# The FFN gates' shifted transfers on the loads' queue, the conv weights loaded spread, the gate products placed between weight splits

## The chip, the cores and the metric

The kernel runs on one core of a Trainium2 chip. The metric is the device time of one execution in microseconds (us); lower is better. One execution of the kernel before was also recorded by the hardware profiler, and all views of the profile below come from that one.

## What is computed

The reference is a decoder trunk of two layers on 256 tokens of width 2048, everything in float32. Layer 0 is a Conformer convolution block, layer 1 an attention block; each is followed by a feed-forward block with a short convolution in its gate. That feed-forward block, with an inner width of 5632, is what the change touches:

```python
def conv_ffn(h, w_in, w_conv, w_out):
    g, u = jnp.split(h @ w_in, 2, axis=-1)
    g = causal_dwconv(g, w_conv)
    return (jax.nn.silu(g) * u) @ w_out

# in each of the two layers, after its convolution or attention block
x = x + conv_ffn(rms_norm(x, ffn_norm_g[layer]), ffn_w_in[layer], ffn_w_conv[layer], ffn_w_out[layer])
```

The convolution is causal and three tokens wide, with one weight for each token distance and column: the gate of token t is a weighted sum of the columns at t, t-1 and t-2.

## The kernel before

**Matrix products.** `linear` (L116 to L165) multiplies the 256 tokens (two halves of 128) by 512 columns of a weight matrix. It walks over the rows of the weights in pairs of 128, a pair being called a chunk here: a 512 KB load into a tile `raw`, issued by SyncE (SP, L134); a ScalarE (ACT) copy that rounds it into the tile `wh` (L138); a VectorE (DVE) subtraction that keeps the rest in `wl` (L144); and twelve TensorE (PE) matmuls, for each of the two rows of the pair and each half of the tokens one with `wh` and the high part of the tokens (L161), one with `wl` (L162) and one with the tokens' low part (L163). `raw`, `wh` and `wl` have four buffers each, so that loads and splits run up to four chunks ahead of the matmuls: a buffer of `wh` or `wl` comes free when the matmuls of the chunk four earlier are done, and a buffer of `raw` when the split of the chunk four earlier is done. A product with 2048 rows has 8 chunks and 96 matmuls.

**The feed-forward block.** `ffn` (L475) runs twice, for l = 0 and l = 1. Its first part goes in 11 groups j of 512 gate columns; each group has two calls of `linear`, one for the gates (`mm_g`, L487) and one for the other half (`mm_u`, L499), so 192 matmuls. Between them stands the convolution along the tokens, which lie on the partitions:

- ACT evicts the gates into `g[0]` (L489, two instructions of 512 columns).
- For the distances d = 1 and 2 the gates are moved down by d partitions into `g[d]`, by three transfers each inside the core's memory (L491, L492, L493): 112 rows, the 15 or 14 that are left, and the d rows that cross from the first half of the tokens to the second. ACT issues all six, on a queue that nothing else uses at that time.
- The 3 x 512 weights of the convolution come as 6 KB into one partition of `wc` on GpSimd's (POOL's) queue (L485), and a GpSimd instruction copies them to all partitions (L486). `wc` has one buffer.
- DVE multiplies `g[1]`, `g[2]` and `g[0]` by their weights (L495) and adds them up (L497), ACT takes the silu (L498), DVE multiplies by the other half (L501), and eight transposes on PE with their splits turn the result for the second part (`turn`, L178, L193, L194).

The second part (L504, L505) multiplies the turned result with `ffn_w_out` in four calls of `linear` with 22 times 2 rows each, and runs `after_ffn0` or `after_ffn1` on each outcome; the latter lets SP issue the stores of the result (L620) between the loads.

**What sets the order.** No order is written out for the FFN. A planner plays the whole program in a model of time as it builds it and puts each instruction into its engine's queue when the model has its inputs and buffers ready; of two that are ready the one that is earlier in the program goes first. Each queue then runs strictly in that order on the chip: an instruction that waits holds up all behind it on its engine, also the transfers that SP or ACT have yet to issue. `tc.issue_after(i)` adds a constraint: what is traced under it on the engine of `i` stands behind `i` in the queue.

Of the kernel before, what the change touches and what calls it, by code (L numbers as in the profile page):

```python
# [10 lines left out]
ALU = mybir.AluOpType  # L11
AX = mybir.AxisListType

P = 128
S = 256
D = 2048
F = 5632
# [9 lines left out]
def kernel(  # L27
# [5 lines left out]
    nc = tc.nc  # L33
# [77 lines left out]
        nc.scalar.activation(warm, ones, AF.Sigmoid)  # L111


    previous = []

    def linear(w, xt, n0, name, lo_engine=None, gain=None, feed=None, nn=512, halves=1, after=None, beside=None,  # L116
               turned=None):

        lo_engine = lo_engine or (lambda c: nc.vector)
        nk = w.shape[0] // P
        acc = ps.tile([P, 2, 512], F32, tag="mm", name=f"mm_{name}", bufs=2)
        wv = w.rearrange("(c p) (h n) -> p c h n", p=P, h=halves)
        for c0 in range(0, nk, 2):
            if feed:
                feed(c0)  # L130
            raw = wp.tile([P, 2, 512], F32, tag="raw", name="raw", bufs=4)[:, :, :nn]
            for h in range(halves):
                k = nn // halves
                nc.sync.dma_start(raw[:, :, h * k:(h + 1) * k], wv[:, c0:c0 + 2, h, n0:n0 + k])  # L134
            wh = wp.tile([P, 2, 512], F32R, tag="wh", name="wh", bufs=4)[:, :, :nn]
            wl = wp.tile([P, 2, 512], F32R, tag="wl", name="wl", bufs=4)[:, :, :nn]
            if gain is None:
                i = nc.scalar.activation(wh, raw, AF.Copy)  # L138
                if beside:
                    with tc.issue_after(i.ins):  # L140
                        beside()
                e = lo_engine(c0 // 2)
                with tc.issue_after(after[e]) if after else ExitStack():
                    i = e.tensor_tensor(wl, raw, wh.bitcast(F32), op=ALU.subtract)  # L144
                if after:
                    after[e] = i.ins
            else:
                for i in range(2):
                    g = prm[:, gain, c0 + i:c0 + i + 1]
                    nc.scalar.activation(wh[:, i, :], raw[:, i, :], AF.Copy, scale=g)  # L150
                    nc.vector.scalar_tensor_tensor(wl[:, i, :], raw[:, i, :], g, wh[:, i, :].bitcast(F32),  # L151
                                                   op0=ALU.mult, op1=ALU.subtract)
            behind = turned if turned and c0 == 4 else previous[0] if turned and c0 == 0 else None
            with tc.issue_after(behind) if behind else ExitStack():
                for i in range(2):
                    c = c0 + i
                    xh, xl = xt[c // 4]
                    for b in range(2):
                        th = xh[:, c % 4, b * P:(b + 1) * P]
                        tl = xl[:, c % 4, b * P:(b + 1) * P]  # L160
                        nc.tensor.matmul(acc[:, b, :nn], th, wh[:, i, :], start=(c == 0), stop=False)  # L161
                        nc.tensor.matmul(acc[:, b, :nn], th, wl[:, i, :], start=False, stop=False)  # L162
                        mm = nc.tensor.matmul(acc[:, b, :nn], tl, wh[:, i, :], start=False, stop=(c == nk - 1))  # L163
        previous[:] = [mm.ins]
        return acc  # L165
# [68 lines left out]
    def project(g, xt, feed=None, beside=None, turned=None):  # L234

        k0, n = GROUPS[g][0] * P, len(GROUPS[g]) * P
        b1 = cp.tile([P, 512], F32, tag="b1", name="b1", bufs=1)
        with tc.high_priority(offset=URGENT):
            acc = linear(conv_w_pw1[0], xt, k0, f"pw1_{g}", lambda c: nc.vector if c in ON_DVE[g] else nc.gpsimd,
                         feed=feed, nn=2 * n, halves=2, beside=beside, turned=turned)  # L240
        for i in range(2):
            nc.sync.dma_start(b1[:, i * n:(i + 1) * n],
                              conv_b_pw1[0:1, i * D + k0:i * D + k0 + n].to_broadcast([P, n]))
        return b1, acc
# [87 lines left out]
    with tc.tile_pool(name="stage", bufs=1) as stage:  # L332
        xt = []
# [8 lines left out]
        def feed(c0):  # L342
            if c0 % 4 == 0:
                xt.append(turn(xg[c0 // 4], G_CONV, xp, "a", c0 // 4))
            elif c0 < 12:
                n = c0 // 4 + 1
                nc.sync.dma_start(xg[n], xv[:, :, n * 512:(n + 1) * 512])
            else:
                turn_taps()
            if c0 == 6:  # L350

                for i, j in ((0, 16), (16, CW)):
                    nc.sync.dma_start(taps[i:j], conv_w_dw[0, i:j])

        b1, acc = project(0, xt, feed)
# [5 lines left out]
    with tc.tile_pool(name="diag", bufs=2) as dp:  # L361
# [18 lines left out]
        def beside():  # L380
            for _ in range(3):
                next(building, None)
# [15 lines left out]
        for g in range(len(GROUPS)):  # L398
            if g:
                b1, acc = project(g, xt, beside=beside if g >= 2 else None, turned=turned)  # L400
# [31 lines left out]
    with tc.tile_pool(name="y", bufs=1) as yp:  # L432
# [25 lines left out]
        xt = []  # L458
        rms = Rms("f0")
        after = {nc.vector: last[0], nc.gpsimd: last_pool[0]}  # L460
        for n in range(NG):
            acc = linear(conv_w_pw2[0], yt, n * 512, f"pw2_{n}",
                         None if n else (lambda c: nc.vector if c < 3 else nc.gpsimd), after=None if n else after)
            b2 = yp.tile([P, 512], F32, tag="b2", name="b2", bufs=2)
            nc.sync.dma_start(b2, conv_b_pw2[0:1, n * 512:(n + 1) * 512].to_broadcast([P, 512]))
            with tc.issue_after(after[nc.gpsimd]):
                nc.gpsimd.tensor_tensor(xg[n], xg[n], b2[:, None, :].to_broadcast([P, 2, 512]), op=ALU.add)
            add_residual(acc, n)
            xt.append(turn(xg[n], G_F0, xp, "a", n))
            rms.add(n)  # L470
# [4 lines left out]
    def ffn(l, xt, r, after):  # L475
        with tc.tile_pool(name=f"h{l}", bufs=1) as hp:

            g = [hp.tile([P, 2, 512], F32, name=f"g{d}") for d in range(3)]
            wc = hp.tile([P, 3, 512], F32, name="wc")
            for d in (1, 2):  # L480
                nc.gpsimd.memset(g[d][:d, 0, :], 0.0)
            ht = []
            for j in range(NJ):
                cols = slice(j * 512, (j + 1) * 512)
                nc.gpsimd.dma_start(wc[0:1], ffn_w_conv[l:l + 1, :, cols])  # L485
                nc.gpsimd.partition_broadcast(wc, wc[0:1])  # L486
                acc = linear(ffn_w_in[l], xt, j * 512, f"g{l}_{j}")  # L487
                for b in range(2):
                    nc.scalar.activation(g[0][:, b, :], acc[:, b, :], AF.Copy, scale=r[:, b:b + 1])  # L489
                for d in (1, 2):  # L490
                    nc.scalar.dma_start(g[d][d:d + 112], g[0][:112])  # L491
                    nc.scalar.dma_start(g[d][d + 112:], g[0][112:P - d])  # L492
                    nc.scalar.dma_start(g[d][:d, 1, :], g[0][P - d:, 0, :])  # L493
                for d in (1, 2, 0):
                    nc.vector.tensor_tensor(g[d], g[d], wc[:, 2 - d:3 - d, :].to_broadcast([P, 2, 512]), op=ALU.mult)  # L495
                for d in (1, 2):
                    nc.vector.tensor_tensor(g[0], g[0], g[d], op=ALU.add)  # L497
                nc.scalar.activation(g[0], g[0], AF.Silu)  # L498
                acc = linear(ffn_w_in[l], xt, F + j * 512, f"u{l}_{j}")  # L499
                for b in range(2):  # L500
                    nc.vector.scalar_tensor_tensor(g[0][:, b, :], acc[:, b, :], r[:, b:b + 1], g[0][:, b, :],  # L501
                                                   op0=ALU.mult, op1=ALU.mult)
                ht.append(turn(g[0], None, hp, "h", j))
            for n in range(NG):  # L504
                acc = linear(ffn_w_out[l], ht, n * 512, f"out{l}_{n}")  # L505
                after(n, acc, g[1 + n % 2])
# [4 lines left out]
    def after_ffn0(n, acc, spare):  # L511
        add_residual(acc, n)
        xt_kv.append(turn(xg[n], None, xp, "a", n))
        rms.add(n)

    ffn(0, xt, r, after_ffn0)
    r = rms.done()


    with tc.tile_pool(name="attn", bufs=1) as ap:  # L520
# [62 lines left out]
        for n in range(NG):  # L583
# [3 lines left out]
            acc = linear(w_kv, xt_kv, D + n * 512, f"v_{n}", gain=G_KV)  # L587
# [6 lines left out]
            for c2 in range(2):  # L594
                po = tp("po")
                for c in range(2):
                    i = 2 * c2 + c
# [7 lines left out]
        xt = []  # L605
        rms = Rms("f1")
        for n in range(NG):
            acc = linear(w_o[0], ot, n * 512, f"o_{n}")
# [7 lines left out]
    def after_ffn1(n, acc, spare):  # L616
        for b in range(2):
            t = spare[:, b, :]
            nc.vector.tensor_tensor(t, acc[:, b, :], xg[n][:, b, :], op=ALU.add)
            nc.sync.dma_start(ov[:, b, n * 512:(n + 1) * 512], t)  # L620

    ffn(1, xt, r, after_ffn1)


# [28 lines left out]
```

## Time and profile before

| | us |
|---|---|
| median of 3 runs | 2202.88 (2202.12 to 2204.95) |
| the profiled execution, its own time | 2218.21 |
| its span, first to last instruction | 2216.4 |

The profiled execution took 15.33 us longer than the median, and 1.8 us of its time lie around the span. How to read it: rows give the time in us from the start of the span, then the duration, the engine, the line of the kernel, and what the instruction writes and reads (`g<-mm_g,r_f` writes tile `g` from `mm_g` and `r_f`); in brackets stands how long the engine was idle before it and what ended that. ACTq and SPq are the sequencers of ACT and SP that issue transfers; such an issue isn't counted as busy time, but the engine's queue goes on only behind it. PE's matmuls are pipelined: a matmul is shown with some 0.39 us, while the next starts 0.23 us after it; PE's pace is therefore read from the starts, and short waits don't show as idle time.

### The profile page before, as it was taken

To read this page: it belongs to the slowest core of one execution; us is meant where nothing else is said; L and a number is where in the kernel's file an instruction comes from. 1 tells how busy PE (TensorE), PEld (TensorE's weight loads), DVE (VectorE), ACT (ScalarE), POOL (GpSimd) and SP (SyncE) were. 2 spreads that over 40 slices of the span, in tenths; PEclk is the share of its full clock that TensorE was granted. 3 is DMA by queue.
4 is the path that set the end of the run, shared out by engine and by line. 5 is a ranking of instruction groups with operands and counts; after the bars stand their busy time and mean duration, and the time that the engine had idled before them with its cause. 6 is when DMAs were issued, how large, how long until landed. Compare 5 with 4: busy or idle time off the path is not lost.

```text
span 2216.4 us, 27040 instructions
## 1 busy us (share of the span) xinstructions
PE 2173.0 (98%) x9951; PEld 1800.9 (81%) x9951; DVE 1395.1 (63%) x1760; ACT 1058.1 (48%) x1443; POOL 303.8 (14%) x207
## 2 busy tenths in 40 slices
PE   8999799999999999999999999999999999999999
PEld 7788688888788888888888888888788888888887
DVE  6999865665666655444566666555666566654443
ACT  6775454444444444444465565544344444443342
POOL 5898501000010000000011001000100000000000
PEclk9999899999999999999999999999999999999999
DMA  7664356777667676555655555567676667766664
GB/s 224 179 205 121 103 192 188 213 215 209 201 209 218 204 211 202 190 190 190 191 182 170 171 177 166 170 187 211 200 218 209 211 198 211 216 208 203 205 201 132
DMA packets 240620, 426.80 MB, mean 193 GB/s; under 512 B 16777, under 2 KB 56091, under 8 KB 240455
## 3 DMA queue, kind: packets, MB, share of 16 engines
q1 hardware_dynamic: 231906, 401.72, 58.5%
q10 hardware_dynamic: 7876, 23.21, 3.9%
q8 instruction: 78, 1.28, 0.2%
q14 instruction: 56, 0.46, 0.1%
q0 software_dynamic: 704, 0.14, 0.0%
HBM read 399.97 MB, written 2.10 MB: 181 GB/s over the span
## 4 chain that ended last, share of the span: by engine, by line
PE 78%; DVE 10%; DMA 7%; issue 2%; ACT 1%; ACTq 1%; POOL 1%; SPq 0%; DVEq 0%; POOLq 0%
PE mm_g L163 7%; PE mm_g L161 7%; PE mm_g L162 7%; PE mm_out L161 7%; PE mm_out L163 7%; PE mm_out L162 7%; DVE acc L281 4%; PE mm_u L162 4%; PE mm_u L163 4%; DMA g<-g 3%; PE mm_u L161 3%; DMA raw<-in_ffn_w_in_dram 2%; DVE wl L144 2%; PE mm_pw L163 2%; PE mm_pw L161 2%
## 5 line engine op out<-in xcount | busy, mean ns | idle before, releaser
L144 DVE TENSOR_TENSOR wl<-raw,wh 128x1024 fp32r<-128x1024 f32 (+1 forms) x595 | 749.1, 1269 | 568.4 <-ACT wh L138 568.4
L138 ACT ACTIVATE wh<-raw 128x1024 fp32r<-128x1024 f32 (+1 forms) x664 | 689.4, 1048 | 815.1 <-PE mm_out L163 272.0
L162 PE MATMUL mm_u<-wl,ah 128*128 128x512 f32 x704 | 276.4, 393 | 11.3 <-DVE wl L144 11.1
L161 PE MATMUL mm_g<-wh,ah 128*128 128x512 f32 x704 | 276.0, 392 | 0.0
L162 PE MATMUL mm_g<-wl,ah 128*128 128x512 f32 x704 | 275.9, 392 | 0.0
L161 PE MATMUL mm_out<-wh,hh 128*128 128x512 f32 x704 | 274.4, 390 | 0.0
L163 PE MATMUL mm_g<-wh,al 128*128 128x512 f32 x704 | 274.3, 390 | 0.0
L163 PE MATMUL mm_out<-wh,hl 128*128 128x512 f32 x704 | 274.2, 389 | 0.0
L162 PE MATMUL mm_out<-wl,hh 128*128 128x512 f32 x704 | 274.1, 389 | 0.0
L163 PE MATMUL mm_u<-wh,al 128*128 128x512 f32 x704 | 274.1, 389 | 0.0
L161 PE MATMUL mm_u<-wh,ah 128*128 128x512 f32 x704 | 274.0, 389 | 0.0
L151 DVE SCALAR_TENSOR_TENSOR wl<-raw,prm,wh 128x512 fp32r<-128x512 f32 x192 | 137.6, 747 | 68.6 <-ACT wh L150 68.4
L150 ACT ACTIVATE wh<-raw,prm 128x512 fp32r<-128x512 f32 x192 | 127.9, 716 | 92.3 <-PE mm_v L163 28.7
L162 PEld LDWEIGHTS mm_u<-wl,ah 128*128 128x128 f32 x704 | 132.1, 188 | 47.1 <-DVE wl L144 20.1
L144 POOL TENSOR_TENSOR wl<-raw,wh 128x1024 fp32r<-128x1024 f32 (+1 forms) x69 | 156.8, 2290 | 36.5 <-ACT wh L138 36.3
L161 PEld LDWEIGHTS mm_u<-wh,ah 128*128 128x128 f32 x704 | 132.2, 188 | 27.8
L163 PEld LDWEIGHTS mm_out<-wh,hl 128*128 128x128 f32 x704 | 132.2, 188 | 27.5
L162 PEld LDWEIGHTS mm_out<-wl,hh 128*128 128x128 f32 x704 | 132.2, 188 | 27.3
L161 PEld LDWEIGHTS mm_out<-wh,hh 128*128 128x128 f32 x704 | 132.2, 188 | 27.1
L163 PEld LDWEIGHTS mm_g<-wh,al 128*128 128x128 f32 x704 | 132.3, 188 | 26.8
L161 PEld LDWEIGHTS mm_g<-wh,ah 128*128 128x128 f32 x704 | 132.2, 188 | 26.8
L163 PEld LDWEIGHTS mm_u<-wh,al 128*128 128x128 f32 x704 | 132.2, 188 | 26.8
(189 smaller groups left out, 3007.1 us busy)
## 6 DMA issues: line engine op xcount, KB each, us to landing
raw<-in_ffn_w_in_dram SPq DMA_DIRECT2D x352, 512.0 KB, 4.1
raw<-in_ffn_w_out_dram SPq DMA_DIRECT2D x176, 512.0 KB, 3.6
raw<-in_w_kv_dram SPq DMA_DIRECT2D x64, 512.0 KB, 3.9
raw<-in_conv_w_pw_dram SPq DMA_DIRECT2D x112, 256.0 KB, 3.0
g<-g ACTq DMA_DIRECT2D x44, 448.0 KB, 4.9
raw<-in_conv_w_pw_dram SPq DMA_DIRECT2D x32, 512.0 KB, 3.6
raw<-in_w_q_dram SPq DMA_DIRECT2D x32, 512.0 KB, 3.6
raw<-in_w_o_dram SPq DMA_DIRECT2D x32, 512.0 KB, 3.7
```

What stands on the lines that cost most here:

```text
L138: i = nc.scalar.activation(wh, raw, AF.Copy)
L144: i = e.tensor_tensor(wl, raw, wh.bitcast(F32), op=ALU.subtract)
L150: nc.scalar.activation(wh[:, i, :], raw[:, i, :], AF.Copy, scale=g)
L151: nc.vector.scalar_tensor_tensor(wl[:, i, :], raw[:, i, :], g, wh[:, i, :].bitcast(F32), op0=ALU.mult, op1=ALU.subtract)
L161: nc.tensor.matmul(acc[:, b, :nn], th, wh[:, i, :], start=(c == 0), stop=False)
L162: nc.tensor.matmul(acc[:, b, :nn], th, wl[:, i, :], start=False, stop=False)
L163: mm = nc.tensor.matmul(acc[:, b, :nn], tl, wh[:, i, :], start=False, stop=(c == nk - 1))
L281: i = nc.vector.scalar_tensor_tensor(a[:, d:], u[:, :S - d], wk, base(k) if d == 0 else a[:, d:], op0=ALU.mult, op1=ALU.add)
```

## The change

In each group of the feed-forward's first part:

- the weights of the convolution are loaded by SP with one transfer that reads the same 3 x 512 values for each of the 128 partitions; POOL's load and its copy to all partitions are gone;
- the six transfers of the shifted gates are issued by SP, the queue of the weights' loads, and no longer by ACT;
- `linear` for the other half is traced before the products of the convolution, and the three products are put behind the sixth, seventh and eighth subtraction (L144) of that `linear`, one behind each. `linear` collects its subtractions in `lows` for this. Adds and silu follow as before.

```diff
-    previous = []
+    previous, lows = [], []
...
         lo_engine = lo_engine or (lambda c: nc.vector)
+        lows.clear()
...
                     i = e.tensor_tensor(wl, raw, wh.bitcast(F32), op=ALU.subtract)
+                lows.append(i.ins)
...
-                nc.gpsimd.dma_start(wc[0:1], ffn_w_conv[l:l + 1, :, cols])
-                nc.gpsimd.partition_broadcast(wc, wc[0:1])
+                nc.sync.dma_start(wc, ffn_w_conv[l:l + 1, :, cols].to_broadcast([P, 3, 512]))
                 acc = linear(ffn_w_in[l], xt, j * 512, f"g{l}_{j}")
...
                 for d in (1, 2):
-                    nc.scalar.dma_start(g[d][d:d + 112], g[0][:112])
-                    nc.scalar.dma_start(g[d][d + 112:], g[0][112:P - d])
-                    nc.scalar.dma_start(g[d][:d, 1, :], g[0][P - d:, 0, :])
-                for d in (1, 2, 0):
-                    nc.vector.tensor_tensor(g[d], g[d], wc[:, 2 - d:3 - d, :].to_broadcast([P, 2, 512]), op=ALU.mult)
+                    nc.sync.dma_start(g[d][d:d + 112], g[0][:112])
+                    nc.sync.dma_start(g[d][d + 112:], g[0][112:P - d])
+                    nc.sync.dma_start(g[d][:d, 1, :], g[0][P - d:, 0, :])
+                acc = linear(ffn_w_in[l], xt, F + j * 512, f"u{l}_{j}")
+
+                for d, low in zip((1, 2, 0), lows[5:]):
+                    with tc.issue_after(low):
+                        nc.vector.tensor_tensor(g[d], g[d], wc[:, 2 - d:3 - d, :].to_broadcast([P, 2, 512]),
+                                                op=ALU.mult)
                 for d in (1, 2):
                     nc.vector.tensor_tensor(g[0], g[0], g[d], op=ALU.add)
                 nc.scalar.activation(g[0], g[0], AF.Silu)
-                acc = linear(ffn_w_in[l], xt, F + j * 512, f"u{l}_{j}")
```

## Rows read from the trace of the kernel before

**Rows 1.** The page, engines: busy time, share of the span, instructions.

```profile
PE 2173.0 (98%) x9951; PEld 1800.9 (81%) x9951; DVE 1395.1 (63%) x1760; ACT 1058.1 (48%) x1443; POOL 303.8 (14%) x207
```

**Rows 2.** Waits of PE, longest first: us in total, times, longest.

```profile
PE mm_u L162 <- DVE wl L144: 11.1, 17, 1.4
```

**Rows 3.** Timeline of PE: first mm_u matmuls of groups, and one group.

```profile
368.88 0.39 PE L161 MATMUL mm_u<-wh,ah 128*128 128x512 f32 x1
...
504.40 0.39 PE L161 MATMUL mm_u<-wh,ah 128*128 128x512 f32 x1
...
518.00 0.39 PE L161 MATMUL mm_u<-wh,ah 128*128 128x512 f32 x1
518.88 0.50 PE L162 MATMUL mm_u<-wl,ah 128*128 128x512 f32 x1 [0.49 <-DVE wl L144]
...
527.17 0.39 PE L162 MATMUL mm_g<-wl,ah 128*128 128x512 f32 x1
...
549.63 0.39 PE L161 MATMUL mm_u<-wh,ah 128*128 128x512 f32 x1
...
822.45 0.39 PE L161 MATMUL mm_u<-wh,ah 128*128 128x512 f32 x1
...
1496.38 0.39 PE L161 MATMUL mm_u<-wh,ah 128*128 128x512 f32 x1
...
1948.71 0.39 PE L161 MATMUL mm_u<-wh,ah 128*128 128x512 f32 x1
```

**Rows 4.** Timeline of DVE in the same group.

```profile
502.97 1.23 DVE L144 TENSOR_TENSOR wl<-raw,wh 128x1024 fp32r<-128x1024 f32 x1 [1.49 <-ACT wh L138]
...
510.89 1.23 DVE L495 TENSOR_TENSOR g<-g,wc 128x1024 f32<-128x1024 f32 x1 [2.82 <-DMA g<-g]
...
515.33 2.36 DVE L495 TENSOR_TENSOR g<-g,wc 128x1024 f32<-128x1024 f32 x2 [2.08 <-DMA g<-g]
517.61 2.35 DVE L144 TENSOR_TENSOR wl<-raw,wh 128x1024 fp32r<-128x1024 f32 x2
```

**Rows 5.** Timeline of ACT and its sequencer in the same group.

```profile
504.60 1.27 ACT L489 ACTIVATE g<-mm_g,r_f 128x512 f32<-128x512 f32 x2 [1.66 <-PE mm_g L163]
505.32 0.55 ACTq L493 DMA_DIRECT2D g<-g  x1
...
509.31 0.65 ACTq L493 DMA_DIRECT2D g<-g  x1
510.08 2.01 ACT L138 ACTIVATE wh<-raw 128x1024 fp32r<-128x1024 f32 x2 [3.26 <-PE mm_u L163]
512.76 1.06 ACT L138 ACTIVATE wh<-raw 128x1024 fp32r<-128x1024 f32 x1 [0.67 <-PE mm_u L163]
```

**Rows 6.** Line L491: from issue to landing; tile g: DVE's waits (us, times).

```profile
DMA to landing us min/median/max: 4.2/4.9/8.4
  DMA g<-g: 107.3, 44
```

**Rows 7.** Issues of transfers by line: count, KB each, median us to landing.

```profile
raw<-in_ffn_w_in_dram SPq DMA_DIRECT2D x352, 512.0 KB, 4.1
b<-in_conv_b_pw_dram SPq DMA_DIRECT2D x4, 256.0 KB, 3.1
```

**Rows 8.** Stretch 482 to 527 us: busy time by engine, clock, DMA share, GB/s.

```profile
482.00:527.00 45.00, 44.51 (x201) 36.58 (x200) 28.48 (x26) 19.47 (x22) 3.07 (x2) 1.00 0.70 209
```

**Rows 9.** SP's sequencer: a load's issue, a wait, and the stores' waits (ns).

```profile
508.10 0.37 SPq L134 DMA_DIRECT2D raw<-in_ffn_w_in_dram  x1
...
SPq L465 <- PE pd L395: 14.9, 1, 14.9
...
L620 SPq EVENT_SEMAPHORE  x6: 17/28/432, 2032.1 to 2092.6; - x6
```

**Rows 10.** POOL's copy of the weights and the subtraction beside it.

```profile
520.20 2.55 POOL L486 PARTITION_BROADCAST wc<-wc  x1 [1.45 <-DMA wc<-in_ffn_w_conv_dram]
521.01 2.68 DVE L144 TENSOR_TENSOR wl<-raw,wh 128x1024 fp32r<-128x1024 f32 x1
```

## The prediction

> **What bounds the kernel now.** I read the engines' busy times first [rows 1]: PE is busy for 98% of the span, at a granted clock of 1.00 in the stretch that I look at [rows 8], the upper of its two levels, 2.4 GHz. So nothing that frees ACT, DVE or POOL is worth anything in itself; the change can only give back time in which PE doesn't start a matmul. PE's waits come next [rows 2]: the largest in the feed-forward stages, and the only one that the change touches, is `mm_u` waiting for `wl`, 17 times, 11.1 us. As short gaps don't show as idle, I then measure PE's pace from the starts [rows 3]. From 504.40 to 518.00 run five chunks of 12 matmuls without a gap: 13.60 / 60 = 0.2267 us each. The stretch of the gates, 527.17 to 549.63, holds 95 matmuls (one of its 96 was run ahead of that) and eight transposes in 22.46 us, so the transposes cost 22.46 - 95 x 0.2267 = 0.92 us. A group without gaps would take 192 x 0.2267 + 0.92 = 44.45 us. Groups do take (822.45 - 368.88) / 10 = 45.36 us in layer 0 and (1948.71 - 1496.38) / 10 = 45.23 us in layer 1. The loss is 0.91 and 0.78 us per group, 16.9 us over the 20 groups between those rows, and with two more groups of 0.85 us 18.6 us in all 22. That is the most that the change can give, 0.8% of the time.
>
> Where the loss arises is seen in one group [rows 3 to 5]. PE stands at 518.00 to 518.88 in front of the first matmul that reads `wl` of the sixth chunk. DVE makes that `wl` only at 517.61, because three gate products stand ahead of it in DVE's queue, and these wait for the shifted gates: 2.82 us before 510.89 and 2.08 us before 515.33. In sum DVE stands 107.3 us for these transfers, 44 times [rows 6]. ACT adds to it: its six issues run from 505.3 to 509.96 (the last starts at 509.31 and takes 0.65), so the `wh` of the fifth and of the sixth chunk start at 510.08, although the buffer of the fifth was free when PE had done the first chunk of `mm_u`, at 504.40 + 2.72 = 507.12.
>
> **Part 1, the products' new place.** The `wh` of the sixth chunk ends at 510.08 + 2.01 = 512.1 [rows 5]; with no product ahead its `wl` would follow that of the fifth, for which DVE is free behind the first product (510.89 + 1.23 = 512.1) and is done at 513.3; it would end at 514.5, while PE wants it at 518.23: 3.7 us early where it was 0.65 late. Chunks pass every 2.72 us (12 x 0.2267) and a subtraction takes 1.23, so that DVE has 1.49 us free in each, as the idle time before 502.97 shows [rows 4]; a product of 1.23 fits into that. The three products keep their cost (none is added or removed); they move off the path. The work behind them (two adds of the products' shape, taken at 1.23 us each, between subtractions, and the silu, of the shape of a `wh` copy and taken at 1.06) then ends near 525, while the `mm_u` sums that it meets end at about 504.4 + 22.0 = 526.4. It gets later by no more than that cover, 1.4 us; if the cover fails, the transposes come late by what is missing.
>
> **Part 2, the six issues on SP.** ACT loses some 4.6 us of issuing per group, so the `wh` copies can follow PE again: that of the seventh starts 0.2 us after PE has done the third chunk (512.76 against 504.40 + 3 x 2.72 = 512.56), and that of the sixth would start so at 510.0, its `wl` end at 510.0 + 1.06 + 1.23 = 512.3 or a little later; the lead over PE grows to 5.8 us. The cost goes to SP. Priced as on ACT the six take the same 4.6 us; a load's issue on SP is 0.37 us [rows 9], so six of these would be 2.2 us; I take 4.6. Behind the eviction (505.87) they run to 510.5. Queued behind them are the loads: the one at 508.10 goes out at 510.5, 2.4 us later. It lands, at 4.1 us [rows 7], near 514.6; its bytes also share the engines with 1.04 MB of gates: at 209 GB/s for a share of 0.70 [rows 8] a full share moves about 300 GB/s, so up to 3.5 us more, 518.1. PE wants that eighth chunk at 504.40 + 7 x 2.72 = 523.4, less 1.06 and 1.23 for its splits: 521.1. The cover is 3.0 us in the worst case. The shifted gates, first issued at about 506.5 and for d = 2 at about 508.5, land 4.9 us later in the median and 8.4 at most [rows 6]: 511.4 and 513.4, at most 514.9 and 516.9. The products behind the sixth and seventh `wl` would come at about 512.4 and 515.1. So in the median no wait, in the worst case 2.5 us, against 5.8 us of lead. I charge nothing; bounds 0 and 0.3 us per group.
>
> The Trainium skill (DMA: Bandwidth & Descriptors, "Issuing engines are not separate DMA queues") says that starting transfers from several engines saves only the sequencers' issuing time, since all run on the same 16 DMA engines. No run here shows yet whether that holds for SP; by that rule the change in landing would be nil and the gain from this part would be ACT's issue time alone.
>
> **Part 3, the weights' load.** POOL's load and its copy (2.55 us) go; the subtraction beside the copy took 2.68 us instead of 1.23 [rows 10]. That comes behind PE's stall, with PE supplied, so I count 0 for the 1.45 us; DVE gains the slack. The new transfer brings 128 x 6 KB = 786 KB per group, 17 MB in all. Its nearest row is the 256 KB load of one vector to all partitions, 3.1 us to landing [rows 7]; three of these in a row would be 9.3 us. It may start when the third product has read `wc`, near 520, and is wanted some 40 us later, so its own time is hidden. It takes up to 786 / 300 = 2.6 us of the engines from the loads behind it, after the burst of gates has been worked off (12 us at 300 against the loads' 188 GB/s make 1.3 MB of room). Cover as above, 3 us or more. Cost 0, bounds 0 and 0.2 us per group. The wait that the change adds to SP, for that third product, holds up loads only if the load behind it was ready earlier; that load waits for the next subtraction on the same engine, DVE, which stands behind the product.
>
> **The sum.** 22 groups x 0.85 = 18.6 us of loss, of which I leave 0.15 us per group for the new small waits: 22 x 0.7 = 15.4, rounded to 15. The profiled execution would go from 2218.2 to 2203. The median was 15.3 us under it; the stalls may be a little smaller without the profiler, which I leave in the range. Forecast 2202.9 - 15 = 2188 us.
>
> **Rivals.** (a) *The lateness only moves.* The shifted gates now share a row of queues with the loads, land later, and the products hold the seventh and eighth `wl` as they held the sixth. For it: the transfers alone took up to 8.4 us [rows 6]. Against it: the lead of 5.8 us; to stall PE as now, the first would have to land near 518, over 6 us later than I reckon, or behind 1.8 MB of other bytes at 300 GB/s, and no more than two loads (1.0 MB) are under way. It would give 2200 to 2206, say 2203. The Trainium skill (same page, "Queues, rings and completion order") speaks for this rival: each DMA engine takes turns between rows and goes through one row in order. By that, gates behind two loads would come some 3.5 us later than on a row of their own, which this trace, where they have one, cannot show.
>
> (b) *SP stands still: slower.* If the planner puts the six issues too far ahead among the loads, SP waits at them for the eviction, and the loads behind are late. Put one or two loads too early, the covers of above take it; from three on it decides: the fifth chunk's load then lands at about 510.5 + 4.1, with 2.3 of splits 517, while PE wants it at 515.3. With the gates' bytes ahead that is 2 to 5 us per group; at 2.6 us x 22 = 57 us the time is 2260. Against it: SP's stores at L620, which also depend on the work behind a `linear`, made SP wait 0.43 us at most ahead of loads [rows 9]. For it: at L465 SP once stood 14.9 us. That is also the price for the first weights' load of each layer, whose buffer must first come free: 14.9 less some 5 us of cover, twice, is 20 us, which with the gain of 15 would be 2208.
>
> (c) *Only a part comes back*, because the profiled execution shows more stall than others, or the silu's chain makes the transposes late by some 0.3 us per group: 2193 to 2199.
>
> **How the numbers follow.** The full gain, 2184 to 2192: 0.60. Rival (c): 0.13. Rival (a): 0.13. Rival (b): 0.14, some of it at 2208 and the rest far above. A measurement of this kernel can tell about 0.2%, 4.4 us, from no change. Below 2198.5 lie the first case and nearly all of (c): 0.73; within, 2198.5 to 2207.3: 0.13; above: 0.14. The range goes from 2183 (18.6 us of loss and 1 us of measurement) up through (c) and half of (a): 2183 to 2203.
>
> **What would show it.** Right: PE's wait `mm_u` for `wl` falls from 11.1 to under 2 us and groups come every 44.4 to 44.7 us; DVE's wait for `g<-g` falls below 30 us; ACT's `wh` copies run every 2.72 us through the start of `mm_u`; POOL loses some 22 x 2.6 = 57 us of its 303.8; SP's waits at L491 to L493 end with the eviction. Wrong: the groups stay at 45.3 us with DVE waiting for `g<-g` behind the sixth subtraction (a); ACT's `wh` waiting for `raw` loads in `mm_u` (b); PE waiting in front of the transposes for L501 (c). What I rely on without a row is where the planner puts SP's new issues among the loads.

## The result and the profile after

The changed kernel takes 2188.47 us in the median (2187.09 to 2192.64), the kernel before in the same comparison 2203.91 us: a ratio of 0.9931, 95% interval 0.9911 to 0.995, 15.4 us less. The forecast was 2188 us, 15 less.

It lies in the groups of the feed-forward blocks. The timeline of PE in the changed kernel, with the same four starts of `mm_u` as in [rows 3] (in this kernel L161 to L163 are L163 to L165):

```profile
355.75 0.39 PE L163 MATMUL mm_u<-wh,ah 128*128 128x512 f32 x1
...
800.12 0.39 PE L163 MATMUL mm_u<-wh,ah 128*128 128x512 f32 x1
...
1473.94 0.39 PE L163 MATMUL mm_u<-wh,ah 128*128 128x512 f32 x1
...
1918.31 0.39 PE L163 MATMUL mm_u<-wh,ah 128*128 128x512 f32 x1
```

Ten groups take 444.37 us in both layers, 44.44 us each, where they took 45.36 and 45.23. The time without gaps was reckoned at 44.45, so PE has no gap left there that the change could close. From the last `mm_u` start of layer 0 shown to the first of layer 1 the two kernels take about the same, 673.82 us (1473.94 - 800.12) against 673.93 (1496.38 - 822.45). The waits of PE no longer have a row for `mm_u` [rows 2], and the waits of DVE none for `g<-g`, which was 107.3 us [rows 6]. The page's engine row, against [rows 1]:

```profile
PE 2158.8 (99%) x9951; PEld 1796.2 (82%) x9951; DVE 1368.5 (63%) x1760; ACT 1066.1 (49%) x1443; POOL 236.1 (11%) x163
```

One group in the timeline of the changed kernel, DVE and SP, against [rows 4, 9]. `mm_u` starts at 489.05; L145 is the subtraction, L499 the product, L494 the first and last of the gates' transfers, L487 the weights' load:

```profile
495.79 1.23 DVE L145 TENSOR_TENSOR wl<-raw,wh 128x1024 fp32r<-128x1024 f32 x1 [1.50 <-ACT wh L139]
496.93 1.22 DVE L499 TENSOR_TENSOR g<-g,wc 128x1024 f32<-128x1024 f32 x1
498.51 1.23 DVE L145 TENSOR_TENSOR wl<-raw,wh 128x1024 fp32r<-128x1024 f32 x1 [0.36 <-ACT wh L139]
499.65 1.22 DVE L499 TENSOR_TENSOR g<-g,wc 128x1024 f32<-128x1024 f32 x1
501.23 1.23 DVE L145 TENSOR_TENSOR wl<-raw,wh 128x1024 fp32r<-128x1024 f32 x1 [0.36 <-ACT wh L139]
502.37 1.22 DVE L499 TENSOR_TENSOR g<-g,wc 128x1024 f32<-128x1024 f32 x1
...
489.97 0.56 SPq L494 DMA_DIRECT2D g<-g  x1
...
493.98 0.76 SPq L494 DMA_DIRECT2D g<-g  x1
494.84 8.01 SPq L135 DMA_DIRECT2D raw<-in_ffn_w_in_dram  x5
503.61 0.37 SPq L487 DMA_DIRECT2D wc<-in_ffn_w_conv_dram  x1
```

The sixth `wl` is done at 497.02, 7.97 us after the start of `mm_u`; PE wants it 13.83 us after (518.23 - 504.40 in the group of before). The products fit into DVE's free time in each chunk and none waits for a transfer. SP waits for the gates' eviction at the first of the six (28.3 us in the 22 groups, 1.3 at most), without harm to PE. It issues the six within 4.8 us, and the next load goes out at 494.84, 5.79 us after the start of `mm_u`, where it went out 3.70 us after (508.10 - 504.40).

The two profiled executions differ by more than the medians, 31.1 us of span. 13.1 us of this lie ahead of the first group (`mm_u` at 368.88 and 355.75) in code that is the same in both; the granted clock over the first 340 us was 0.95 there and 0.98 here. A second profile of the kernel before, below, lost 7.8 us less in that stretch. The text therefore compares times of groups, in which the granted clock is 1.00, the upper level, but for the few cases named.

### The profile page after: what moved, and what is told of

Its sections match the earlier page's. It is cut to its first block, busy times and chain, and to the rows that moved or that the text cites. A ratio compares the mean times of both kernels' runs of the same rounds, so it can differ in the third digit from the quotient of the medians.

```text
span 2185.3 us, 27016 instructions
## 1 busy us (share of the span) xinstructions
PE 2158.8 (99%) x9951; PEld 1796.2 (82%) x9951; DVE 1368.5 (63%) x1760; ACT 1066.1 (49%) x1443; POOL 236.1 (11%) x163
## 4 chain that ended last, share of the span: by engine, by line
PE 91%; DVE 8%; DMA 1%; issue 0%; SPq 0%; POOL 0%; ACT 0%; DVEq 0%; ACTq 0%; POOLq 0%
PE mm_g L165 7%; PE mm_out L165 7%; PE mm_g L164 7%; PE mm_g L163 7%; PE mm_u L164 7%; PE mm_u L163 7%; PE mm_out L164 7%; PE mm_u L165 7%; PE mm_out L163 7%; DVE acc L283 5%; PE mm_pw L165 2%; PE mm_pw L163 2%; PE mm_pw L164 2%; PE ptx L180 1%; PE mm_v L165 1%; PE mm_v L163 1%
## 5 line engine op out<-in xcount | busy, mean ns | idle before, releaser
L145 DVE TENSOR_TENSOR wl<-raw,wh 128x1024 fp32r<-128x1024 f32 (+1 forms) x595 | 726.4, 1222 | 666.9 <-ACT wh L139 666.9
L139 ACT ACTIVATE wh<-raw 128x1024 fp32r<-128x1024 f32 (+1 forms) x664 | 696.8, 1050 | 882.3 <-PE mm_out L165 274.2
L165 PE MATMUL mm_g<-wh,al 128*128 128x512 f32 x704 | 276.2, 392 | 0.0
L163 PE MATMUL mm_g<-wh,ah 128*128 128x512 f32 x704 | 276.1, 392 | 0.0
L165 PE MATMUL mm_out<-wh,hl 128*128 128x512 f32 x704 | 274.5, 390 | 0.0
L163 PE MATMUL mm_out<-wh,hh 128*128 128x512 f32 x704 | 274.5, 390 | 0.0
L165 PE MATMUL mm_u<-wh,al 128*128 128x512 f32 x704 | 274.0, 389 | 0.0
L163 PE MATMUL mm_u<-wh,ah 128*128 128x512 f32 x704 | 274.0, 389 | 0.0
L145 POOL TENSOR_TENSOR wl<-raw,wh 128x1024 fp32r<-128x1024 f32 (+1 forms) x69 | 157.5, 2301 | 26.8 <-ACT wh L139 26.8
L163 PEld LDWEIGHTS mm_u<-wh,ah 128*128 128x128 f32 x704 | 132.2, 188 | 27.4
L165 PEld LDWEIGHTS mm_u<-wh,al 128*128 128x128 f32 x704 | 132.2, 188 | 27.4
L163 PEld LDWEIGHTS mm_out<-wh,hh 128*128 128x128 f32 x704 | 132.2, 188 | 27.2
L165 PEld LDWEIGHTS mm_out<-wh,hl 128*128 128x128 f32 x704 | 132.2, 188 | 27.1
L164 PEld LDWEIGHTS mm_g<-wl,ah 128*128 128x128 f32 x704 | 132.3, 188 | 26.7
L165 PEld LDWEIGHTS mm_g<-wh,al 128*128 128x128 f32 x704 | 132.2, 188 | 26.8
```

## Experiments

The question was which of three edits does it, and why. Theory P was the prediction's main line: the products stood ahead of the sixth subtraction in DVE's queue and waited there for the gates. Theory Q was its second: ACT, held by six issues, made its copies late. A further theory, H, came up on the way and is stated where it is tested. Of the runs whose name begins with "pinned" or "loads" and of the second profile there is one execution each, so they are judged by their groups and not by their total time.

**The second profile of before.** No edit.

> The kernel before, profiled once more. If the first profiled execution lost its extra 13 us ahead of the first feed-forward stage by chance (TensorE at its lower clock there), the first mm_g matmul now starts near 333 instead of 346 us and the span is near 2202, with the loss in the groups as before, 17 to 19 us in all. If the profiler makes it, both stay at 346 and 2216.

It took 2207.93 us. PE's timeline:

```profile
361.04 0.39 PE L161 MATMUL mm_u<-wh,ah 128*128 128x512 f32 x1
...
812.74 0.39 PE L161 MATMUL mm_u<-wh,ah 128*128 128x512 f32 x1
...
1487.52 0.39 PE L161 MATMUL mm_u<-wh,ah 128*128 128x512 f32 x1
...
1938.07 0.39 PE L161 MATMUL mm_u<-wh,ah 128*128 128x512 f32 x1
```

Groups of 45.17 and 45.06 us: a loss of 0.73 and 0.62 us, 14.9 us over 22 groups, where the first profile had 18.6. So the size of the loss itself differs between executions, and my expectation of 17 to 19 was too narrow; the stretch ahead of the groups is partly shorter (361.04 against 368.88), so its length is an execution's own.

**The products' place alone.** The changed kernel with the weights' load and all six transfers back as they were before:

```diff
-                nc.sync.dma_start(wc, ffn_w_conv[l:l + 1, :, cols].to_broadcast([P, 3, 512]))
+                nc.gpsimd.dma_start(wc[0:1], ffn_w_conv[l:l + 1, :, cols])
+                nc.gpsimd.partition_broadcast(wc, wc[0:1])
...
-                    nc.sync.dma_start(g[d][d:d + 112], g[0][:112])
+                    nc.scalar.dma_start(g[d][d:d + 112], g[0][:112])
...
```

> The kernel before with the products' new place alone; the transfers stay on ACT's queue, the weights with POOL. Theory P (the loss arises since the products stand ahead of the sixth subtraction and wait there for the shifted gates): groups take 44.4 to 44.6 us, PE's wait of mm_u for wl is under 1 us, the time is that of the whole change, 2186 to 2191 us. Theory Q (the loss arises since ACT is held by six issues, so that its copies are late): ACT's copies are as late as before, groups stay at 45.2 to 45.4 us, 2202 to 2206 us.

2190.99 us, a ratio of 0.9943 (0.9925 to 0.9961); groups of 44.45 and 44.44 us. The timeline, PE, ACT and DVE:

```profile
492.68 0.39 PE L163 MATMUL mm_u<-wh,ah 128*128 128x512 f32 x1
...
498.30 2.01 ACT L139 ACTIVATE wh<-raw 128x1024 fp32r<-128x1024 f32 x2 [3.20 <-PE mm_u L165]
...
499.39 2.36 DVE L145 TENSOR_TENSOR wl<-raw,wh 128x1024 fp32r<-128x1024 f32 x2 [3.04 <-ACT wh L139]
501.67 1.22 DVE L500 TENSOR_TENSOR g<-g,wc 128x1024 f32<-128x1024 f32 x1
```

ACT's copies are as late as before, 5.62 us after the start of `mm_u` (5.68 in [rows 5]), yet the sixth `wl` ends at 501.75, 9.07 us after it and 4.8 us ahead of PE. P is enough by itself.

**The transfers' queue alone.** The kernel before, with all six transfers on SP:

```diff
-                    nc.scalar.dma_start(g[d][d:d + 112], g[0][:112])
+                    nc.sync.dma_start(g[d][d:d + 112], g[0][:112])
...
```

> The kernel before with the six transfers issued by SP, nothing else. Theory P: the products still stand ahead of the sixth subtraction and wait for transfers that land no earlier than before; groups stay at 45.1 to 45.5 us, DVE's wait for the shifted gates stays near 100 us, 2201 to 2208 us. Theory Q: groups of 44.4 to 44.6 us, 2186 to 2191 us.

2190.99 us, 0.9934 (0.9915 to 0.9952); groups of 44.53 (one of 45.18, the others 44.45 to 44.59) and 44.44 us. This is what theory Q expected and P excluded, though the products still stand ahead of the sixth subtraction (in this timeline and some of the next, the last two lines are the first and the last group of layer 1: 444.37 us for ten groups here):

```profile
492.01 0.39 PE L161 MATMUL mm_u<-wh,ah 128*128 128x512 f32 x1
...
498.39 1.23 DVE L495 TENSOR_TENSOR g<-g,wc 128x1024 f32<-128x1024 f32 x1 [1.14 <-DMA g<-g]
500.67 2.36 DVE L495 TENSOR_TENSOR g<-g,wc 128x1024 f32<-128x1024 f32 x2 [1.05 <-DMA g<-g]
502.95 1.22 DVE L144 TENSOR_TENSOR wl<-raw,wh 128x1024 fp32r<-128x1024 f32 x1
...
1477.80 0.39 PE L161 MATMUL mm_u<-wh,ah 128*128 128x512 f32 x1
...
1922.17 0.39 PE L161 MATMUL mm_u<-wh,ah 128*128 128x512 f32 x1
```

The second product starts 8.66 us after the start of `mm_u`; before it was 10.93 (515.33 - 504.40). So either edit takes the loss away, and the second one by something that I had not counted: the gates of d = 2 land 2.3 us earlier. But the planner had also put one more subtraction ahead of the first product, and ACT was free as well. Three causes are mixed.

**The weights' load alone.** The kernel before, with

```diff
-                nc.gpsimd.dma_start(wc[0:1], ffn_w_conv[l:l + 1, :, cols])
-                nc.gpsimd.partition_broadcast(wc, wc[0:1])
+                nc.sync.dma_start(wc, ffn_w_conv[l:l + 1, :, cols].to_broadcast([P, 3, 512]))
```

> The kernel before with the weights' load spread over the partitions by SP, nothing else. Theories P and Q alike: no change, 2201 to 2207 us, groups 45.1 to 45.4 us; POOL loses 57 us of busy time and one subtraction per group 1.4 us, both beside the path. Rival: the 786 KB per group delay the loads behind them, groups over 45.6 us, 2210 us or more.

2206.14 us, 0.9998 (0.9984 to 1.0013), groups of 45.22 and 45.27 us: this part neither gives nor costs anything that these runs can tell, in spite of its 17 MB. SP's waits in this run show that it does make SP stand for the third product, without harm:

```profile
SPq L485 <- DVE g L494: 79.2, 20, 4.9
```

In the changed kernel that wait is 13.8 us, 0.7 at most.

**Separating the three causes.** In the next four runs the order of the products on DVE is written out as it was before, so that the planner can't move them; weights stay with POOL. Their expectations call theory Q "A", and "L" the theory that on the loads' own queue the gates go ahead of the next load. First the base, which is also the control. `products` runs ahead of each chunk of `mm_u` and puts one product ahead of the fifth subtraction and two ahead of the sixth:

```diff
+                chain = {nc.vector: lows[-1]}
+                def products(c0):
+                    for d in {8: (1,), 10: (2, 0)}.get(c0, ()):
+                        with tc.issue_after(chain[nc.vector]):
+                            i = nc.vector.tensor_tensor(g[d], g[d], ..., op=ALU.mult)
+                        chain[nc.vector] = i.ins
+                acc = linear(ffn_w_in[l], xt, F + j * 512, f"u{l}_{j}", feed=products, after=chain)
```

> The order of the products in DVE's queue is written out as it was before (one behind the fourth subtraction of mm_u, two behind the fifth, the sixth behind those); transfers on ACT's queue, weights with POOL. A control for the next three: groups of 45.0 to 45.4 us as before, a loss of 0.6 to 0.9 us in each, 2201 to 2208 us.

2202.04 us; groups of 44.87 and 45.09 us. A smaller loss than in the two profiles of before (0.43 and 0.65 us), but it is there. Its timeline, PE, SP and DVE:

```profile
538.45 0.39 PE L163 MATMUL mm_u<-wh,ah 128*128 128x512 f32 x1
...
542.15 0.37 SPq L135 DMA_DIRECT2D raw<-in_ffn_w_in_dram  x1
...
545.22 1.23 DVE L501 TENSOR_TENSOR g<-g,wc 128x1024 f32<-128x1024 f32 x1 [3.09 <-DMA g<-g]
...
549.71 2.36 DVE L501 TENSOR_TENSOR g<-g,wc 128x1024 f32<-128x1024 f32 x2 [2.13 <-DMA g<-g]
...
1481.99 0.39 PE L163 MATMUL mm_u<-wh,ah 128*128 128x512 f32 x1
...
1932.84 0.39 PE L163 MATMUL mm_u<-wh,ah 128*128 128x512 f32 x1
```

Now the same with the transfers on SP (`nc.sync` in place of `nc.scalar`):

> The same written order, with the six transfers on SP's queue. Theories L (on the loads' own queue the gates go ahead of the next load, and land 2 us earlier) and A (ACT is no longer held by the issues) both expect groups of 44.4 to 44.6 us. If the gain of the transfers' queue alone came only from the planner's new order of the products, the groups stay at 45.0 us or more.

2189.48 us; groups of 44.45 and 44.44 us.

```profile
535.62 0.39 PE L163 MATMUL mm_u<-wh,ah 128*128 128x512 f32 x1
...
541.34 7.25 SPq L135 DMA_DIRECT2D raw<-in_ffn_w_in_dram  x3
...
542.42 1.22 DVE L501 TENSOR_TENSOR g<-g,wc 128x1024 f32<-128x1024 f32 x1 [3.12 <-DMA g<-g]
...
544.70 2.35 DVE L501 TENSOR_TENSOR g<-g,wc 128x1024 f32<-128x1024 f32 x2
```

The first product starts at the same distance from the start of `mm_u` as in the control, 6.80 against 6.77 us; the other two start at 9.08 instead of 11.26. The planner's order is ruled out as the only cause. Next, ACT is held again by dummy work where the issues stood; `hold` has the last dummy copy:

```diff
+                for _ in range(6):
+                    junk = work.tile([P, 512], F32, tag="junk", name="junk", bufs=1)
+                    held = nc.scalar.activation(junk, g[0][:, 1, :], AF.Copy)
...
+                with tc.issue_after(hold[0]) if hold and c0 == 8 else ExitStack():
                     i = nc.scalar.activation(wh, raw, AF.Copy)
```

> As pinned_sp, and ACT is held for some 4 us by six dummy copies at the place where the six issues stood (the copy wh of the fifth chunk is written behind them). Theory L: the gates still land near 8 us after the start of mm_u, the sixth subtraction ends before 12.8 us, groups stay at 44.4 to 44.6 us. Theory A: the loss is back, groups of 45.0 us or more.

2196.31 us, with groups of 44.45 and 44.44 us; what it takes longer than the run before lies ahead of the groups (`mm_u` first starts at 364.62, there at 357.84). ACT and DVE:

```profile
542.40 0.39 PE L164 MATMUL mm_u<-wh,ah 128*128 128x512 f32 x1
...
544.70 3.95 ACT L495 ACTIVATE junk<-g 128x512 f32<-128x512 f32 x6
548.56 2.00 ACT L140 ACTIVATE wh<-raw 128x1024 fp32r<-128x1024 f32 x2
...
551.39 2.35 DVE L506 TENSOR_TENSOR g<-g,wc 128x1024 f32<-128x1024 f32 x2
```

The copies start 6.16 us after the start of `mm_u`, later than the 5.68 us of before, and no loss comes back. Holding ACT makes no loss as long as the gates land early; the next run shows that freeing it takes none away. Theory Q falls: ACT's issuing time is worth nothing here. And with ACT free but the transfers on a queue of their own again, POOL's (`nc.gpsimd`):

> As pinned_sp, with the six transfers on POOL's queue: ACT is as free as with SP, and the transfers take turns with the loads again. Theory L: the last gates land 10 us or more after the start of mm_u, the products wait for them, groups of 45.0 us or more. Theory A: 44.4 to 44.6 us.

2213.01 us; groups of 45.31 and 45.42 us (45.09 without one of 48.36, in which the granted clock fell to 0.50, the lower level, for 3.4 us, right behind a stop in front of the fifth `wl`, 2.4 us from one start of PE to the next).

```profile
542.60 0.39 PE L163 MATMUL mm_u<-wh,ah 128*128 128x512 f32 x1
...
550.03 1.23 DVE L501 TENSOR_TENSOR g<-g,wc 128x1024 f32<-128x1024 f32 x1 [3.76 <-DMA g<-g]
...
553.29 2.36 DVE L501 TENSOR_TENSOR g<-g,wc 128x1024 f32<-128x1024 f32 x2 [0.89 <-DMA g<-g]
```

ACT is free and the loss is there in full; the last two products start 10.69 us after the start of `mm_u`. (From POOL the first large packets move 3.4 us after the start of `mm_u`, from ACT or SP 2.8 us after it, medians of 22 groups.) With the products in this order, the time at which the gates land decides.

**Why they land earlier from SP.** Two ways were left. Either it matters that transfers and loads share a queue, or (theory H) SP, busy with issuing, simply sends the next load out later: 5.72 us after the start of `mm_u` (541.34) instead of 3.70 (542.15 in the control). The test has the transfers on ACT's queue, and SP kept busy by six tiny transfers:

```diff
+                for i in range(6):
+                    nc.sync.dma_start(idle[2 * i:2 * i + 2], g[0][2 * i:2 * i + 2, 1, :64])
```

> As pinned_act (the products in the order of before, the gates' transfers on ACT's queue), and SP issues six tiny transfers (2 rows of 64 columns of the gates into a tile that nothing reads) at the place where the gates' issues stand in the changed kernel, so that the next load goes out some 2 us later, as it does there. Theory H (the gates land earlier on SP's queue because SP, busy with their issues, holds the next load back): the products for d = 2 and 0 start near 9 us after the start of mm_u instead of 11.3, groups of 44.4 to 44.6 us, 2188 to 2193 us. Theory R (it is the sharing of one row of queues that matters): they still start at 10.5 us or later, groups of 44.8 to 45.3 us, 2196 to 2206 us.

2194.12 us; groups of 44.45 and 44.46 us. PE, SP and DVE:

```profile
540.30 0.39 PE L163 MATMUL mm_u<-wh,ah 128*128 128x512 f32 x1
...
541.79 4.99 SPq L494 DMA_DIRECT2D idle<-g  x6
546.88 2.65 SPq L135 DMA_DIRECT2D raw<-in_ffn_w_in_dram  x2
...
549.05 2.35 DVE L504 TENSOR_TENSOR g<-g,wc 128x1024 f32<-128x1024 f32 x2
...
1480.91 0.39 PE L163 MATMUL mm_u<-wh,ah 128*128 128x512 f32 x1
...
1925.49 0.39 PE L163 MATMUL mm_u<-wh,ah 128*128 128x512 f32 x1
```

The load goes out 6.58 us after the start of `mm_u`, the last two products start 8.75 us after it, and the loss is gone, with the gates on their own queue and ACT held by its issues. Theory H holds: one load, sent out in the middle of the six issues, was what made the gates late. The packets of the trace show it, in KB that begin to move in each us from 2 to 10 us after the start of `mm_u`, in the groups shown above and in the mean of all 22 groups:

```
                              2    3    4    5    6    7    8    9
pinned_act          gates    24  241  196   57   36  233  172   65
                    load(s) 316   11   26   67  249  118   24   30
pinned_act_sp_held  gates     0  258  270  274  217   16    0    0
                    load(s) 329    6    0    0    0   24  169  329
pinned_sp           gates    36  249  262  286  167   32    0    0
                    load(s) 294    6    0    0   32  200  294    0
mean of 22 groups:
pinned_act          gates    27  238  254  134  118  120  114   29
                    load(s) 313    5    6   29  113  208  112   76
pinned_act_sp_held  gates     1  241  276  251  225   41    0    0
                    load(s) 311    6    0    0    0   34  189  282
```

In the control's group shown, the load takes most of the microsecond from 6 to 7, between the gates for d = 1 and d = 2. Seven of its 22 groups look like that. In the other 15 the gates for d = 2 have begun by then; there the load takes most of the microsecond from 7 to 8 (199 to 291 KB), in which the gates move 41 to 111 KB, so that it holds up their last part. In both kinds the last gates land late. The load's own bytes aren't all of the delay: from 5 to 6 us gates and load together move 163 KB in the mean, the gates alone 251 KB where the load is held back. Why is not shown. By the same packets the last byte of the gates is moved 10.1 us after the start of `mm_u` in the second profile of before (median of 22 groups), and 7.8 us after in the changed kernel.

**Transfers too early in SP's queue: rival (b).** The changed kernel, with the loads from the sixth, or from the fifth chunk of `mm_u` on written behind the six transfers (m = 5 and 4; `hold` has the last transfer):

```diff
+                with tc.issue_after(hold[0]) if hold and c0 >= 2 * m else ExitStack():
                     nc.sync.dma_start(raw[:, :, h * k:(h + 1) * k], wv[:, c0:c0 + 2, h, n0:n0 + k])
```

> The whole change, with the loads of the sixth, seventh and eighth chunk of mm_u written behind the six transfers on SP's queue; as planned, only the eighth stands behind them, so the transfers stand two loads too early. Rival (b) as priced in the prediction (covers take up to two loads): groups of 44.4 to 44.9 us, 2186 to 2199 us. If SP's wait costs in full what it delays the loads by (the sixth from 2.5 us before mm_u's start to 5.8 us after it), groups go over 47 us, 2245 us or more.

2191.86 us; groups of 44.47 and 44.44 us: two loads too early cost nothing.

> The same with the fifth load behind the transfers too, three loads too early. As priced in the prediction: the fifth load goes out 5.8 us after the start of mm_u, lands behind the gates near 11 us, its splits take 2.3 us more, PE wants it at 11.1 us: 2 to 5 us lost per group, groups of 46.5 to 49.5 us, 2233 to 2300 us, most likely 2243. If PE's four chunks of cover took it, groups would stay under 45 us.

2241.06 us; groups of 46.37 and 46.99 us. In four of the 20, of 48.2 to 48.4 us, the granted clock falls to 0.50, the lower level, for 3.4 us each, right behind PE's waits for the fifth chunk; without them it is 46.14 and 46.41, a loss of 1.7 and 2.0 us. The timeline, PE, SP, ACT and DVE:

```profile
498.71 0.39 PE L164 MATMUL mm_u<-wh,ah 128*128 128x512 f32 x1
...
504.63 1.41 SPq L136 DMA_DIRECT2D raw<-in_ffn_w_in_dram  x3
...
509.24 1.06 ACT L140 ACTIVATE wh<-raw 128x1024 fp32r<-128x1024 f32 x1 [8.12 <-DMA raw<-in_ffn_w_in_dram]
...
510.33 1.23 DVE L146 TENSOR_TENSOR wl<-raw,wh 128x1024 fp32r<-128x1024 f32 x1 [7.95 <-ACT wh L140]
```

The fifth load goes out 5.9 us after the start of `mm_u`, ACT's copy waits until 10.5 us after it, the `wl` ends 12.9 us after it; PE wants it 11.1 us after. The 1.8 us between the two are nearly all of what this group loses (46.37 - 44.44 = 1.9).

## Why the prediction was right, step by step

- *The bound and the loss.* Right: PE sets the end, and a group without gaps takes 44.44 us (44.45 reckoned). The loss of 18.6 us was true of the profiled execution; another one of the same kernel lost 14.9. I left 0.15 us per group (3.3 us) for new waits, and there are none. The two errors of 3 to 4 us point in opposite directions, so it is luck that the 15 us hit more closely than the terms deserve. The 15.3 us by which the profiled execution exceeded the median were not the profiler's price: the second profiled execution of the same kernel took 2207.93 us.
- *Part 1, the products' place.* Right in mechanism and size: alone it gives the whole gain, with a lead of 4.8 us where 3.7 was reckoned (the reckoning left the first product ahead of the fifth subtraction, where the change has none); in the changed kernel the lead is 13.83 - 7.97 = 5.9 us where 5.8 was reckoned. The silu behind the products, which was to get later, ends earlier: 19.2 us after the start of `mm_u` in the group shown, 21.5 in the group of before.
- *Part 2, the issues on SP.* Priced right (4.6 us of issuing, a load 2.4 us late and covered: measured 4.8 and 2.1), but read wrongly. "ACT adds to it" was a step that failed: held for as long as before, ACT costs nothing. And the delay of the load, which I booked as a cost to be covered, is what lets the gates land 2.3 us earlier; that alone takes the loss away. The prediction gave the transfers on SP the landing time that they had on ACT's queue (4.9 us in the median [rows 6], for d = 2 9.0 us after the start of `mm_u`, where 7.8 was measured) and counted no gain from it.
- *The rules cited.* The Trainium skill (DMA: Bandwidth & Descriptors, "Issuing engines are not separate DMA queues") says that issuing from several engines saves only issuing time; by that, ACT's time would have been the gain of part 2. The traces differ: that time is worth 0, and the place of the issues in SP's order takes the whole loss away (14.9 us in the second profile) when it is changed alone. The Trainium skill (same page, "Queues, rings and completion order") says that each DMA engine takes turns between rows and goes through one row in order; that spoke for rival (a), in which gates on the loads' row land later. They land earlier, since the load that they would have to share with has not yet been sent.
- *Part 3, the weights' load.* Right: 0. The share of the DMA engines rose from 0.70 at 209 GB/s [rows 8] to 0.74 at 229 (482 to 527 us in both traces) without a wait of PE behind it. SP's wait for the third product is 0.7 us at most, so the 20 us that rival (b) put on the first load of each layer did not come. POOL lost 67.7 us of busy time against 57 forecast; I had left out its 22 issues of 0.5 us.
- *Rivals.* (b) was priced at 2.6 us per group from the third load on; measured are 0 at two loads and 1.7 to 2.0 at three. The time of that run, 2241 us, was brought to where it was expected, 2243, with the help of the lower clock. (a) did not show: DVE has no wait for the gates left in the changed kernel. Of (c), the transposes come on time in every group; that the profiled execution showed more loss than others was true by 3.7 us (18.6 against 14.9), which the 3.3 us left for new waits made up for.

## What to carry to other kernels

This stall was held up by two props, an instruction that stands too early in a queue and a transfer that lands too late; to know which edit pays, take each one alone: here either does the whole. A wait that one engine pays on its own queue can be a gain: SP's delay of one load by 2 us let six urgent transfers through. Price a transfer put into a loads' queue by how many loads it passes: as long as the prefetch covers them it is free (two loads here); the third cost 1.7 to 2.0 us in each group.

## What the runs showed of the hardware

- A 512 KB load, sent from SP while ACT was issuing two sets of three transfers (0.52 MB each), was served ahead of the second set or of its last part: in the 22 groups of the control it moved 176 to 291 KB in the microsecond in which it moved most, and the gates 4 to 111. A queue of their own did not put the gates ahead of a load that was sent during their issuing; the last byte came 2.3 us later (10.1 us after the start of `mm_u` in the second profile of before, 7.8 in the changed kernel).
- A load of 3 x 512 values to 128 partitions (786 KB, read from the same 6 KB) ran beside 8.4 MB of loads per group, at 229 GB/s in all, without delaying PE.
- The lower clock in a group of the feed-forward began right behind a stop of PE in all five cases (four with the fifth load late, one with POOL issuing), lasted 3.4 us, and matmuls then started every 0.43 us instead of 0.23. Most groups with such stops kept the upper clock.
- The same program lost between 14.9 and 18.6 us in the same 22 groups in two executions, and 361 or 369 us passed ahead of the first `mm_u`; a difference of a few microseconds between single executions of this kernel says nothing.
